# One weight block in four unsplit at the head of the channel mixers, and the norm's bias added later

## The chip, the cores and the metric

The kernel runs on one core of a Trainium2 chip, in one launch. The metric is the device time of the launch in microseconds, the median of the runs shown. TensorE multiplies matrices, DVE (VectorE) and POOL (GpSimd) work elementwise, ACT (ScalarE) applies functions, scales and biases, and SP issues the DMAs. Each engine works through its own queue in order.

## The reference

Two decoder layers over 256 tokens of width 2048, all in float32. Every sub-layer ends in `x = LayerNorm(alpha * x + sublayer(x))`, `LayerNorm(x) = (x - mean) / sqrt(var + eps) * g + b`. What matters here is the border between a mixer and the channel mixer that follows it:

```
x = layer_norm(ALPHA * x + mixer(x), ln1_g, ln1_b)
gate, val = x @ w_gate, x @ w_val            # 2048 -> 5632 each
h = silu(causal_dwconv(gate, conv_w) + conv_b) * val
x = layer_norm(ALPHA * x + h @ w_down, ln2_g, ln2_b)
```

## The kernel before

**Layout.** Activations lie feature-major: 16 tiles of 128 features x 256 tokens. The residual is `xf[0..15]` in float32. Weights come from memory as one stream per phase, in 128x128 blocks in the order of use; a chunk is eight blocks (512 KB), loaded by one DMA on SP's queue into one of three buffers (tag `wr`, L251).

**Three passes.** A float32 product is made of three TensorE passes in the faster type float32r. Each operand is split exactly into two parts, w = hi + lo and x = xh + xl, and a block is `hi xh + lo xh + hi xl` (`mac`, L350 to L354). `Stream.take` splits half a chunk (four blocks, 512 columns) at a time: ACT copies it to `wh` (L261), DVE or POOL subtracts to get `wl` (L265). There are four buffers of each. A raw buffer is free again when both its halves are split.

**The end of a mixer.** `out_part(..., last=True)` adds the last rows of the output projection to the residual (L848), tile by tile, and for each tile `ln_tile` (L402) takes the square on ACT, the sum of x on POOL (`accE`, L415) and the sum of the squares on DVE (`accQ`, L416). `ln_sums` (L420) then sums over the partitions with one-column matmuls (`lnst`, L433), gets 1/std on DVE, and spreads mean and 1/std over the partitions (`lnb`).

**The lead.** So as not to wait for these sums, the first nine groups of the channel mixer (`LEADS = 9`: a group of four column blocks, gate and value, then eight of one; 192 weight blocks in each layer) multiply the input before its LayerNorm, scaled by g: `raw(i)` makes the split of g x (`rawh` on ACT, L531; on POOL g x again, L534, and `rawl`, L535), with g and b in two more columns, so these matmuls have 258 columns. `plain` (L547) turns each result into that of the normalised input, with two DVE operations and two of ACT. Meanwhile `apply(i)` (L475) normalises the 16 tiles for the groups behind the lead: POOL subtracts the mean (L469), DVE multiplies by g and 1/std (L470) and adds the bias into the residual (`shift`, L473), ACT makes `xh` (L480) and POOL `xl` (L481). Two of these stand in each of the later lead groups (`PACE`), ordered behind the weight splits issued before them.

**What sets the order.** The program is written in the order of the code, and a planner reorders the instructions of each engine before the launch by modelled times and priorities; `tc.high_priority` moves the sums and the residual forward. On the chip each engine then keeps that order. In the lead, one in four of the splits goes to POOL (`LWL = "vvvp"`), after the first group.

**Behind the lead** come 38 column groups of gate and value blocks on `xh`, `xl`, each with the convolution (L636 to L638), the gate (L639, L640) and a split of the hidden tile (L324, L325), and then the down projection (`psd`), which adds to the residual (L656).

Of the kernel before, what the change touches and what calls it, by code (L numbers as in the profile page):

```python
# [9 lines left out]
F32 = mybir.dt.float32  # L10
# [6 lines left out]
P = 128  # L17
# [12 lines left out]
# ------------------------------------------------------------------ weight streams  # L30
# Each phase reads its weights as one stream of 128x128 blocks in the order of use.
# [93 lines left out]
# ------------------------------------------------------------------ small parameters  # L125
# [43 lines left out]
# ------------------------------------------------------------------ constants of the shapes  # L169
# [59 lines left out]
# ------------------------------------------------------------------ the program  # L229
class Stream:  # L230
    """The weights of a phase, in blocks of 128x128 in the order of use, split exactly into two parts
    of 12 significant bits: w = hi + lo."""
# [7 lines left out]
    def take(self, w, kt, key, n=1):  # L240
# [13 lines left out]
        if r == 0:  # L254
            self.hi = k.wpool.tile([P, self.HALF * P], F32R, name=f"wh_{self.name}_{c}_{g}", tag="wh", bufs=k.NWS)
            self.lo = k.wpool.tile([P, self.HALF * P], F32R, name=f"wl_{self.name}_{c}_{g}", tag="wl", bufs=k.NWS)
        sub = k.SUB.get(self.name, self.HALF)
        if r % sub == 0:
            a = slice(r * P, (r + sub) * P)
# [11 lines left out]
class K:  # L271
# [7 lines left out]
    # ---- set-up  # L279
# [25 lines left out]
    def need(self, kt, ahead=1):  # L305
        """Emit what makes tiles up to kt of the phase's input, and a few beyond."""
        while self.make_x and KT - len(self.make_x) <= kt + ahead:
            self.make_x.pop(0)()
# [21 lines left out]
    def phase(self, ctx, name, **banks):  # L330
        """The PSUM banks of a phase, by use."""
# [17 lines left out]
    # ---- three passes of exactly split operands  # L349
    def mac(self, out, hi, lo, xh, xl, first, last):  # L350
        mm = self.nc.tensor.matmul
        mm(out, hi, xh, start=first, stop=False)  # L352
        mm(out, lo, xh, start=False, stop=False)  # L353
        mm(out, hi, xl, start=False, stop=last)  # L354
# [11 lines left out]
    # ---- s -> 1/sqrt(s)  # L366
# [6 lines left out]
    def rsqrt_half(self, pool, h, n, name, ch=0):  # L373
        """h = -s / 2 -> 1/sqrt(s)."""
# [12 lines left out]
    # ---- residual + LayerNorm, feature-major  # L387
    def ln_start(self, name):
# [3 lines left out]
        if name[0] == "m":  # L392
            raw = self.lnctx.enter_context(self.tc.tile_pool(name=f"raw_{name}", **right))
            self.raw = [raw.tile([P, KT, T + 2], F32R, name=f"raw{n}_{name}") for n in "hl"]
        self.lnsum = ExitStack()
# [6 lines left out]
    def ln_tile(self, name, i):  # L402
        """Sums of x and x^2 over the feature tiles but for the last few, which ln_finish adds."""
# [16 lines left out]
    def ln_sums(self, name):  # L420
        """-> the mean and 1 / std of each token, spread over the partitions; yields between the two steps."""
# [4 lines left out]
        # the means of x and x^2 over the features, for the two halves of the tokens  # L426
# [23 lines left out]
        with hp(self.HP):  # L450
            v.tensor_copy(mean, st[0])
            # var = max(E[x^2] - mean^2, 0) + eps
# [10 lines left out]
    def ln_finish(self, name, gname, bname, final=False):  # L463
# [11 lines left out]
        def apply(i):  # L475
            h, l = self.xh[i], self.xl[i]
            scaled(i, nc.gpsimd)
            if name[0] == "m":
                shift(i)
                nc.scalar.activation(h, self.xf[i], AF.Copy)  # L480
                nc.gpsimd.tensor_tensor(l, self.xf[i], h.bitcast(F32), ALU.subtract)  # L481
                return
            nc.scalar.activation(h, self.xf[i], AF.Identity, bias=self.p(bname, i))
            v.scalar_tensor_tensor(l, self.xf[i], self.p(bname, i), h.bitcast(F32), ALU.add, ALU.subtract)
            if i == KT - 1:
                self.lead_done()
# [36 lines left out]
        # The products that come first take g x, before its LayerNorm, with g and b in two more columns  # L523
        rh, rl = self.raw
        gb = self.p(gname, 0, 2 * KT).rearrange("p (a k) -> p k a", a=2)
        nc.scalar.activation(rh[:, :, T:], gb, AF.Copy)
        v.tensor_tensor(rl[:, :, T:], gb, rh[:, :, T:].bitcast(F32), ALU.subtract)

        def raw(i):
            h, l = rh[:, i, :T], rl[:, i, :T]  # L530
            nc.scalar.activation(h, self.xf[i], AF.Copy, scale=self.p(gname, i))  # L531
            if i % 4 in self.RAWP:
                t = self.lnp.tile([P, T], F32, name=f"lnr_{name}_{i}", tag="lnr", bufs=2)
                nc.gpsimd.tensor_scalar(t, self.xf[i], self.p(gname, i), 1.0, ALU.mult, ALU.mult)  # L534
                nc.gpsimd.tensor_tensor(l, t, h.bitcast(F32), ALU.subtract)  # L535
            else:
                v.scalar_tensor_tensor(l, self.xf[i], self.p(gname, i), h.bitcast(F32), ALU.mult, ALU.subtract)
# [9 lines left out]
        def plain(o, i):  # L547
            """From W (g x), W g and W b to W (g (x - mean) / std + b)."""
# [7 lines left out]

        def end():
            self.need(KT)

# [15 lines left out]
    RAWP = (0, 1, 2, 3)  # L575

    def lead(self, st, keys, outs):
        """Products of the input of the FFN; the first few are of the input before its LayerNorm, so that they
        do not wait for its sums."""
# [8 lines left out]
        for kt in range(KT):  # L588
# [10 lines left out]
            for (w, key), o in zip(keys, outs):  # L599
                hi, lo = st.take(w, kt, key)  # L600
                self.mac(o[:, :T + 2], hi, lo, self.raw[0][:, kt], self.raw[1][:, kt], kt == 0, kt == KT - 1)
# [6 lines left out]
    def lead_done(self):  # L608
        """The temporaries of lead may go."""
# [4 lines left out]
    # ---- ConvGLU channel mixer  # L614
    def ffn(self, l):
# [3 lines left out]
        with ExitStack() as ctx:  # L619
# [5 lines left out]
            for grp in ffn_groups(l):  # L625
                outs = [self.bank("mm", f"ps_{w}_{c}") for w, c in grp]
                ps.update(zip(grp, self.lead(st, grp, outs)))
                for (w, c) in grp:
# [11 lines left out]
                    v.tensor_tensor(m, s, u, ALU.mult)  # L640
                    if c == FT // 2:
# [18 lines left out]
    # ---- rotary tables for 64-wide heads, two heads to a tile  # L660
    def rope_tables(self, tile):
        """tile(name, dtype) gives the temporaries."""
# [1034 lines left out]
```

## Time and profile before

| | |
|---|---|
| median of 3 runs | 2561.82 us (2561.67 to 2564.18) |
| profiled execution, first to last instruction | span 2556.7 us |
| what lies around the span, by the median | 5.1 us |
| busy share of the span: PE, DVE, ACT, POOL | 96%, 68%, 52%, 21% |
| mean granted TensorE clock | 0.982 of full speed |
| lead of layer 0 | 531.92 to 627.28 us |
| lead of layer 1 | 1769.65 to 1862.16 us |

The page gives no other time of the profiled execution than its span. The busy shares are means over the whole span; the lead is under a tenth of it, and there the shares are others. A matmul's own length in the trace (0.28 us) holds its way through the array; matmuls overlap, and the pace is the distance from start to start.

### The profile page before, as it was taken

What the parts mean: (1) busy time and instruction counts of PE and PEld (TensorE: products, weight loads), DVE (VectorE), ACT (ScalarE), POOL (GpSimd) and SP (SyncE); (2) the same over time, 40 slices, a digit from 0 to 9 for tenths busy, and PEclk for the clock granted to TensorE, in tenths of its full rate; (3) what the DMA queues carried; (4) which work ended last, traced back from release to release, by engine and by line L of the source; (5) the groups of instructions that cost most, each with busy time, mean ns of one, the idle gap of its engine ahead of it and who ended that gap; (6) DMA issues with size and microseconds to landing.
All of it is one profiled execution on the core that took longest, in us unless ns stands there. A gap on an engine that the chain in (4) does not pass through costs nothing.

```text
span 2556.7 us, 52762 instructions
## 1 busy us (share of the span) xinstructions
PE 2447.7 (96%) x20612; PEld 2362.1 (92%) x20612; DVE 1737.3 (68%) x3579; ACT 1328.5 (52%) x2577; POOL 535.8 (21%) x656
## 2 busy tenths in 40 slices
PE   8999999888999999999979999998899999999997
PEld 7888888778999999999979888998899999999996
DVE  6777667769666666555578787758976666665555
ACT  6455454355555555544445454445555555554443
POOL 3333343275000000000044233237500000000001
PEclk9999999989999999999989999999999999999998
DMA  6332333334555555555534444544355555555553
GB/s 214 128 99 89 110 98 117 110 101 147 191 189 190 190 187 187 187 190 190 190 126 147 139 135 146 186 163 159 124 190 190 190 186 188 189 190 190 188 188 128
DMA packets 129417, 412.13 MB, mean 161 GB/s; under 512 B 25488, under 2 KB 30224, under 8 KB 129168
## 3 DMA queue, kind: packets, MB, share of 16 engines
q1 hardware_dynamic: 129168, 408.77, 48.9%
q8 instruction: 161, 2.64, 0.4%
q14 instruction: 88, 0.72, 0.1%
HBM read 405.04 MB, written 2.10 MB: 159 GB/s over the span
## 4 chain that ended last, share of the span: by engine, by line
PE 81%; DVE 11%; issue 2%; DMA 2%; ACT 2%; POOL 1%; SPq 1%; DVEq 0%; ACTq 0%; POOLq 0%
PE psd L353 6%; PE psd L352 6%; PE psd L354 6%; PE ps_l_ffn_w_val L353 6%; PE ps_l_ffn_w_val L354 6%; PE ps_l_ffn_w_val L352 6%; PE ps_l_ffn_w_gate L354 6%; PE ps_l_ffn_w_gate L352 6%; PE ps_l_ffn_w_gate L353 6%; PE pso L352 2%; PE pso L353 2%; PE pso L354 2%; DVE wl_m L265 1%; DVE xf L470 1%; DVE wl_f L265 1%
## 5 line engine op out<-in xcount | busy, mean ns | idle before, releaser
L265 DVE TENSOR_TENSOR wl_f<-wr_f,wh_f 128x512 fp32r<-128x512 f32 x1040 | 744.8, 717 | 523.7 <-ACT wh_f L261 523.1
L261 ACT ACTIVATE wh_f<-wr_f 128x512 fp32r<-128x512 f32 x1056 | 665.8, 632 | 639.0 <-PE psd L354 232.8
L261 ACT ACTIVATE wh_m<-wr_m 128x512 fp32r<-128x512 f32 x464 | 289.8, 629 | 251.4 <-PE pso L354 78.4
L353 PE MATMUL psd<-hh,wl_f 128*128 128x256 f32 x1408 | 393.0, 279 | 0.0
L352 PE MATMUL psd<-hh,wh_f 128*128 128x256 f32 x1408 | 392.8, 279 | 0.0
L354 PE MATMUL psd<-hl,wh_f 128*128 128x256 f32 x1408 | 392.8, 279 | 0.0
L352 PE MATMUL ps_l_ffn_w_gate<-xh,wh_f 128*128 128x256 f32 x1216 | 339.2, 279 | 0.0
L354 PE MATMUL ps_l_ffn_w_gate<-xl,wh_f 128*128 128x256 f32 x1216 | 339.2, 279 | 0.0
L353 PE MATMUL ps_l_ffn_w_val<-xh,wl_f 128*128 128x256 f32 x1216 | 339.2, 279 | 0.0
L354 PE MATMUL ps_l_ffn_w_val<-xl,wh_f 128*128 128x256 f32 x1216 | 339.2, 279 | 0.0
L353 PE MATMUL ps_l_ffn_w_gate<-xh,wl_f 128*128 128x256 f32 x1216 | 339.2, 279 | 0.0
L352 PE MATMUL ps_l_ffn_w_val<-xh,wh_f 128*128 128x256 f32 x1216 | 339.2, 279 | 0.0
L265 POOL TENSOR_TENSOR wl_m<-wr_m,wh_m 128x512 fp32r<-128x512 f32 x154 | 215.0, 1396 | 374.3 <-ACT wh_m L261 308.7
L265 DVE TENSOR_TENSOR wl_m<-wr_m,wh_m 128x512 fp32r<-128x512 f32 x310 | 222.2, 719 | 75.7 <-ACT wh_m L261 68.4
L353 PEld LDWEIGHTS psd<-hh,wl_f 128*128 128x128 f32 x1408 | 264.7, 188 | 0.0
L354 PEld LDWEIGHTS psd<-hl,wh_f 128*128 128x128 f32 x1408 | 264.7, 188 | 0.0
L352 PEld LDWEIGHTS psd<-hh,wh_f 128*128 128x128 f32 x1408 | 264.6, 188 | 0.0
L352 PEld LDWEIGHTS ps_l_ffn_w_val<-xh,wh_f 128*128 128x128 f32 x1216 | 228.6, 188 | 0.0
L353 PEld LDWEIGHTS ps_l_ffn_w_val<-xh,wl_f 128*128 128x128 f32 x1216 | 228.6, 188 | 0.0
L354 PEld LDWEIGHTS ps_l_ffn_w_val<-xl,wh_f 128*128 128x128 f32 x1216 | 228.6, 188 | 0.0
L353 PEld LDWEIGHTS ps_l_ffn_w_gate<-xh,wl_f 128*128 128x128 f32 x1216 | 228.6, 188 | 0.0
L352 PEld LDWEIGHTS ps_l_ffn_w_gate<-xh,wh_f 128*128 128x128 f32 x1216 | 228.6, 188 | 0.0
(637 smaller groups left out, 5578.4 us busy)
## 6 DMA issues: line engine op xcount, KB each, us to landing
wr_f<-w_f SPq DMA_DIRECT2D x526, 512.0 KB
wr_m<-w_m SPq DMA_DIRECT2D x230, 512.0 KB
xf<-x SPq DMA_DIRECT2D x7, 256.0 KB
rwl<-lora SPq DMA_DIRECT2D x8, 192.0 KB
rdt<-rdecay SPq DMA_DIRECT2D x4, 384.0 KB
y<-xf SPq DMA_DIRECT2D x5, 256.0 KB
wr_m<-w_m SPq DMA_DIRECT2D x4, 256.0 KB
wr_f<-w_f SPq DMA_DIRECT2D x4, 256.0 KB
```

The lines of the kernel that those rows point to most:

```text
L261: nc.scalar.activation(self.hi[:, a], raw, AF.Copy)
L265: i = eng.tensor_tensor(self.lo[:, a], raw, self.hi[:, a].bitcast(F32), ALU.subtract)
L352: mm(out, hi, xh, start=first, stop=False)
L353: mm(out, lo, xh, start=False, stop=False)
L354: mm(out, hi, xl, start=False, stop=last)
L470: v.scalar_tensor_tensor(self.xf[i], self.xf[i], self.p(gname, i), rb, ALU.mult, ALU.mult)
```

## The change

In the lead, every fourth block of a half chunk is not split. `take(..., whole=True)` returns the raw float32 block in the loaded chunk, and `mac` multiplies it in one matmul with float32 g x (`rawf`, a third tile of 16 x 258 columns). ACT and DVE or POOL split only the other three blocks, 384 columns.

`raw(i)` makes g x in float32 on ACT, then `rawh` from it on ACT, and POOL only subtracts. `apply(i)` has for both kinds of norm the same form: the bias goes into `xh` on ACT and into `xl` with one DVE operation, and no longer into the residual. The residual gets it from ACT in `late`, one tile for each column group from the 22nd on.

```
-    def take(self, w, kt, key, n=1):
+    def take(self, w, kt, key, n=1, whole=False):
...
+        if whole and r == self.HALF - 1:
+            return self.raw[:, (g * self.HALF + r) * P:(g * self.HALF + r + 1) * P], None
         sub = k.SUB.get(self.name, self.HALF)
         if r % sub == 0:
-            a = slice(r * P, (r + sub) * P)
+            a = slice(r * P, (r + sub - whole) * P)
...
-    def mac(self, out, hi, lo, xh, xl, first, last):
+    def mac(self, out, hi, lo, xh, xl, first, last, x=None):
         mm = self.nc.tensor.matmul
+        if lo is None:
+            mm(out, hi, x, start=first, stop=last)
+            return
...
+            self.rawf = raw.tile([P, KT, T + 2], F32, name=f"rawf_{name}")
...
         def apply(i):
             h, l = self.xh[i], self.xl[i]
             scaled(i, nc.gpsimd)
-            if name[0] == "m":
-                shift(i)
-                nc.scalar.activation(h, self.xf[i], AF.Copy)
-                nc.gpsimd.tensor_tensor(l, self.xf[i], h.bitcast(F32), ALU.subtract)
-                return
             nc.scalar.activation(h, self.xf[i], AF.Identity, bias=self.p(bname, i))
             v.scalar_tensor_tensor(l, self.xf[i], self.p(bname, i), h.bitcast(F32), ALU.add, ALU.subtract)
-            if i == KT - 1:
+            if name[0] == "f" and i == KT - 1:
                 self.lead_done()
...
+        nc.scalar.activation(rf[:, :, T:], gb, AF.Copy)
...
         def raw(i):
-            h, l = rh[:, i, :T], rl[:, i, :T]
-            nc.scalar.activation(h, self.xf[i], AF.Copy, scale=self.p(gname, i))
-            if i % 4 in self.RAWP:
-                t = self.lnp.tile([P, T], F32, name=f"lnr_{name}_{i}", tag="lnr", bufs=2)
-                nc.gpsimd.tensor_scalar(t, self.xf[i], self.p(gname, i), 1.0, ALU.mult, ALU.mult)
-                nc.gpsimd.tensor_tensor(l, t, h.bitcast(F32), ALU.subtract)
-            else:
-                v.scalar_tensor_tensor(l, self.xf[i], self.p(gname, i), h.bitcast(F32), ALU.mult, ALU.subtract)
+            f, h, l = rf[:, i, :T], rh[:, i, :T], rl[:, i, :T]
+            nc.scalar.activation(f, self.xf[i], AF.Copy, scale=self.p(gname, i))
+            nc.scalar.activation(h, f, AF.Copy)
+            nc.gpsimd.tensor_tensor(l, f, h.bitcast(F32), ALU.subtract)
...
+        def late(i):
+            nc.scalar.activation(self.xf[i], self.xf[i], AF.Identity, bias=self.p(bname, i))
+
         def end():
             self.need(KT)
+            self.late = [lambda i=i: late(i) for i in range(KT)]
...
-                hi, lo = st.take(w, kt, key)
-                self.mac(o[:, :T + 2], hi, lo, self.raw[0][:, kt], self.raw[1][:, kt], kt == 0, kt == KT - 1)
+                hi, lo = st.take(w, kt, key, whole=True)
+                self.mac(o[:, :T + 2], hi, lo, self.raw[0][:, kt], self.raw[1][:, kt], kt == 0, kt == KT - 1,
+                         self.rawf[:, kt])
...
+                    if c >= FT // 2 and self.late:
+                        self.late.pop(0)()
```

## Rows read from the trace of the kernel before

**Rows 1.** The page's first part: busy us, share of the span, instructions.

```profile
PE 2447.7 (96%) x20612; PEld 2362.1 (92%) x20612; DVE 1737.3 (68%) x3579; ACT 1328.5 (52%) x2577; POOL 535.8 (21%) x656
```

**Rows 2.** Stretches: length, busy us (instructions) by engine, clock, DMA share, GB/s.

```profile
565.00:625.00 60.00, 50.23 (x385) 47.01 (x384) 59.08 (x94) 35.90 (x85) 39.55 (x38) 1.00 0.40 132
1800.00:1860.00 60.00, 52.87 (x397) 49.79 (x395) 58.54 (x95) 35.84 (x85) 37.94 (x38) 0.97 0.42 137
531.00:560.00 29.00, 23.86 (x169) 23.25 (x170) 15.47 (x34) 9.96 (x20) 24.58 (x30) 0.88 0.40 128
...
640.00:660.00 20.00, 20.00 (x174) 20.00 (x173) 12.39 (x22) 11.23 (x20) 0.00 (x0) 1.00 0.61 205
```

**Rows 3.** Timeline of PE at the lead's begin and end: start, length.

```profile
531.92 0.28 PE L352 MATMUL ps_l_ffn_w_gate<-rawh_m,wh_f 128*128 128x258 f32 x1
...
532.28 0.28 PE L352 MATMUL ps_l_ffn_w_val<-rawh_m,wh_f 128*128 128x258 f32 x1
...
627.28 0.28 PE L352 MATMUL ps_l_ffn_w_gate<-xh,wh_f 128*128 128x256 f32 x1
```

**Rows 4.** Timeline of PE at the norm's sums, idle time before in brackets.

```profile
552.80 1.01 PE L433 MATMUL lnst_m<-cb,accE_m 128*128 128x1 f32 x4 [4.49 <-POOL accE_m L415]
...
556.23 0.56 PE L352 MATMUL ps_l_ffn_w_gate<-rawh_m,wh_f 128*128 128x258 f32 x1
...
1786.91 0.61 PE L433 MATMUL lnst_m<-cb,accE_m 128*128 128x1 f32 x4 [3.79 <-POOL accE_m L415]
```

**Rows 5.** A stretch of 3 us behind that wait, columns as above.

```profile
556.00:559.00 3.00, 3.00 (x15) 3.00 (x16) 1.57 (x8) 0.63 (x1) 0.00 (x0) 0.50 0.00 0
```

**Rows 6.** Timeline of PE: two float32 matmuls among split ones, layer 1.

```profile
1389.49 1.02 PE L1419 MATMUL gq<-KQ 128*128 128x256 f32 x4
...
1390.47 0.28 PE L352 MATMUL psz<-xh,wh_m 128*128 128x256 f32 x1
```

**Rows 7.** Weight loads of that line: ns min/median/max, first and last start.

```profile
L1419 PEld LDWEIGHTS gq<-KQ x16: 187/188/191, 1382.1 to 1523.4; 128*128 128x128 f32 x16
```

**Rows 8.** DVE by line, 565 to 625: busy us, mean ns, idle before.

```profile
L265 DVE TENSOR_TENSOR wl_f<-wr_f,wh_f 128x512 fp32r<-128x512 f32 x21 | 16.0, 771 | 0.0
L473 DVE TENSOR_SCALAR xf<-xf,pb 128x256 f32<-128x256 f32 x16 | 13.1, 821 | 0.0
L470 DVE SCALAR_TENSOR_TENSOR xf<-xf,pb,lnb_m 128x256 f32<-128x256 f32 x16 | 11.1, 696 | 0.8 <-ACT lnb_m L447 0.8
L637 DVE SCALAR_TENSOR_TENSOR fa<-lnp_m_l_ffn_w_gate,pb,fa 128x255 f32<-128x255 f32 x5 | 4.3, 861 | 0.0
...
L325 DVE TENSOR_TENSOR hl<-fm,hh 128x256 fp32r<-128x256 f32 x5 | 3.2, 633 | 0.0
```

**Rows 9.** DVE by line, 1800 to 1860.

```profile
L473 DVE TENSOR_SCALAR xf<-xf,pb 128x256 f32<-128x256 f32 x16 | 8.3, 520 | 0.1
```

**Rows 10.** POOL by line, 565 to 625.

```profile
L481 POOL TENSOR_TENSOR xl<-xf,xh 128x256 fp32r<-128x256 f32 x16 | 16.9, 1064 | 9.1 <-ACT xh L480 8.0 <-ACT lnuv_m_l_ffn_w_gate L551 1.1
```

**Rows 11.** Four lines: ns min/median/max, first and last start us.

```profile
L534 POOL TENSOR_SCALAR lnr_m<-xf,pb x16: 468/650/1432, 515.6 to 554.5; 128x256 f32<-128x256 f32 x16
...
L484 DVE SCALAR_TENSOR_TENSOR xl<-xf,pb,xh x16: 468/471/1509, 1314.9 to 1333.2; 128x256 fp32r<-128x256 f32 x16
...
L470 DVE SCALAR_TENSOR_TENSOR xf<-xf,pb,lnb_m x16: 471/476/1519, 565.4 to 621.3; 128x256 f32<-128x256 f32 x16
...
L265 DVE TENSOR_TENSOR wl_f<-wr_f,wh_f x21: 677/680/1216, 570.5 to 620.7; 128x512 fp32r<-128x512 f32 x21
```

**Rows 12.** Timeline of DVE: an undisturbed 256-column operation.

```profile
526.91 0.41 DVE L416 TENSOR_TENSOR accQ_m<-accQ_m,lnq_m 128x256 f32<-128x256 f32 x1
```

**Rows 13.** SP's issue of a weight load, and the stretch in which its data ends.

```profile
562.24 0.33 SPq L251 DMA_DIRECT2D wr_f<-w_f  x1
...
565.00:566.00 1.00, 1.00 (x10) 1.00 (x10) 0.62 (x2) 1.00 (x4) 0.13 (x1) 1.00 0.42 66
```

More of the change, by code (lines that the diff above doesn't have):

```diff
@@ L524, in ln_finish @@
         rh, rl = self.raw
+        rf = self.rawf
         gb = self.p(gname, 0, 2 * KT).rearrange("p (a k) -> p k a", a=2)
+        nc.scalar.activation(rf[:, :, T:], gb, AF.Copy)
         nc.scalar.activation(rh[:, :, T:], gb, AF.Copy)
@@ L574 @@
     FIND = (1, 2, 3, 4, 6, 8, 10, 12, 14, 15, 16)
-    RAWP = (0, 1, 2, 3)
     def lead(self, st, keys, outs):
```

## The prediction

> **What bounds the kernel now.** I read the totals first: TensorE is busy 96% of the span [rows 1]. That means that a microsecond is won only where TensorE stands still or runs slowly, and any extra TensorE work costs time everywhere else. So I next cut the span into stretches. In the body of a channel mixer, 20 us hold 174 matmuls and DVE works 12.4 of them: TensorE sets the pace, 0.115 us a matmul [rows 2]. The change touches another stretch, the first 192 weight blocks of each channel mixer (the lead, nine groups). It begins at 531.92 and ends at 627.28 in layer 0, 95.4 us [rows 3]. Its three matmuls of 258 columns a block need 0.36 us (531.92 to 532.28), so 192 blocks need 69 us. Some 26 us are lost, in two places.
>
> Place A is the LayerNorm's sums, at 531 to 565. POOL runs without a break there (24.6 of 29 us [rows 2], the rest is after its last sum). TensorE waits 4.49 us for the last sum of x (3.79 us in layer 1) [rows 4]; behind that wait its granted clock is 0.50, the 1.2 GHz level [rows 5], so the sixteen one-column matmuls take 3.4 us (552.80 to 556.23) and the blocks behind them run at half pace.
>
> Place B is the normalisation beside the other groups: 565 to 625 and, in layer 1, 1800 to 1860. DVE is busy 59.1 and 58.5 of 60 us, TensorE issues 385 and 397 matmuls where 500 would fit [rows 2]. Here DVE sets the end: every block needs its lo half from DVE's queue, in which the normalisation's work stands too.
>
> **The change part by part.** The terms are against the profiled execution: its span is 2556.7 us; the median of the runs, 2561.8, lies 5.1 us above the span, which I carry over unchanged.
>
> *TensorE.* Of 384 lead blocks 96 go unsplit. The matmul of two float32 operands is visible elsewhere: two of 256 columns are four instructions, and from their first to the second split matmul behind them are 0.98 us [rows 6]. Less one split matmul (0.12) that is 0.43 us each, 0.44 at 258 columns, against 0.36: +0.08 a block, +7.7 us over both layers where TensorE sets the pace. No further gap is seen at the switch. Both weight loads of such a pair take 188 ns, as any other [rows 7], and lie beside its matmuls. The Trainium skill, "TensorE: Matmul & The Clock Gate", section "Weight-path perf modes", says that the fast weight load is not used for FP32; its formula (128 columns at 1.2 GHz) gives an estimate of 107 ns for a load, and if those loads lay bare, 96 x 2 x 0.107 = 20.6 us would be added and the change would lose. The trace does not agree that they do: 0.98 us leaves them no room.
>
> *Splits on DVE and ACT.* They shrink from 512 to 384 columns. A 256-column subtraction takes 0.41 [rows 12], a 512-column one 0.68 [rows 11], so 384 take 0.55: -0.13 each at least, a quarter of the mean 0.771 (-0.19) at most. I take the first: 21 of them in B [rows 8], -2.8 us, 23 in layer 1, -3.1.
>
> *Normalisation.* The bias addition leaves DVE (16 x 0.821 = 13.1 us in layer 0, 16 x 0.520 = 8.3 in layer 1 [rows 8, 9]). In its place stands the three-operand subtraction that POOL did. The channel mixers' own LayerNorm has that form: median 471 ns, longest 1509 [rows 11]; the bounds are 16 x 0.471 = 7.5 and, at the mean of the scaling beside it [rows 8], 16 x 0.696 = 11.1. I take the middle, 9.3: -3.8 us in layer 0, +1.0 in layer 1.
>
> *POOL gets out of DVE's way.* POOL loses 16.9 us of xl subtractions [rows 10], of 39.6 busy in B. DVE's operations are long only at times: the scaling has a median of 476 ns, a mean of 696 and a longest of 1519 [rows 8, 11]. Time over the undisturbed length: 21 x 0.09 for splits, 16 x 0.22 for scalings, and 20 convolution and gating operations (861 the first, 633 the last group) over 0.47, 20 x 0.28; together 11 us. Bounds: all or none goes. I let it fall with POOL's busy time, 43%: -4.7 us a layer. The Trainium skill, "SBUF — State Buffer", section "SBUF: two separate sides", says why such a thing could be: DVE and GpSimd share one port pair as an exclusive lock, and a DVE operation with two SBUF inputs takes part in it against a GpSimd operation that reads SBUF. By that rule the new DVE subtraction is exposed as the old addition was, and could cost its upper bound; the 1509 ns in rows 11 agrees.
>
> *B together.* DVE: 59.1 - 2.8 - 3.8 - 4.7 = 47.8 us, and 58.5 - 3.1 + 1.0 - 4.7 = 51.7. TensorE for the same 128 and 132 blocks: three quarters at 0.36, one at 0.44, 48.6 and 50.2 us. The two are now equal, so what is late next is TensorE itself, and two in-order queues with equal work never overlap fully. I choose 10% over the larger: 53.5 and 56.9, a gain of 6.5 + 3.1 = 9.6 us. Ends: no such loss, 19.7; 20%, -0.3.
>
> *A.* POOL loses the scaling of each tile, 16 with a median of 0.65 us [rows 11], over 10 us of the chain that ends in the late sum. It can't all come off: the place of the sums in TensorE's order is planned from modelled times, which see POOL shorten as well, so the wait may only move forward. All of it is worth 4.5 + 1.7 (the sums at full clock) + 1.5 (blocks at half pace, half of the 3 us in rows 5) = 7.7 us in layer 0, 6.8 in layer 1; none is the other end. I take a third, 4.8, less 31 whole blocks x 0.08 = 2.5: -2.3 us net (-12 to +2.5).
>
> *Costed at nothing.* ACT gets 16 more copies a layer for the unscaled split (about 0.4 us each). They lie in 531 to 560, where ACT is busy 10 of 29 us [rows 2]; without that cover 16 x 0.4 = 6.5 us a layer. The 16 late bias additions on ACT stand one to a column group in the body, where ACT works 11.2 of 20 us [rows 2] and nothing reads the residual until the down projection; without cover 16 x 0.5 = 8 us. Nothing of layer 1's input waits for them. No DMA is moved.
>
> *A wait is added.* A raw chunk (three buffers) was free when its split was done; now also TensorE must have passed its eighth block. Behind that wait stand only later weight loads on SP's queue. Issue to landing: issued at 562.24, the transfer ends in 565 to 566 [rows 13], 3 us. Round trip: 3.0 + hi 0.6 + lo 0.6 + the chunk itself (6 x 0.36 + 2 x 0.44 = 3.0) = 7.3 us in the time of three chunks, 9.1. 1.8 us are spare; I cost it at nothing.
>
> Sum: -9.6 - 2.3 = -11.9; 2556.7 - 11.9 + 5.1 = 2549.9, so 2550 us.
>
> **The rivals.**
> *The sums' wait goes, and the queues overlap well.* For it: POOL's chain loses more than twice the wait. Against: the planned order. -19.7 - 12 = -31.7 us: 2530.
> *DVE's relief is eaten.* For it: DVE's long operations may come from the POOL work that stays (the mean subtractions and the split in four), and equal queues stall. B gives nothing (+0.3), A +2.5 to -2: 2561 to 2565, no change that can be told. Against: at least 2.8 and 3.1 us of splits are gone for certain.
> *Slower: the raw chunk is held too long.* Mechanism: the late load holds ACT's hi split, that holds DVE's in-order queue, and with it the normalisation. It decides once queueing on ACT and DVE passes the spare 1.8 us a round. In B, DVE has 94 instructions in 60 us, so a split stands behind several of 0.5 to 0.9; with 4 us of queueing each chunk takes (4 - 1.8)/3 = 0.73 us longer, over the 32 chunks of B +23 us. With the -11.9: +11, 2573. For it: prefetch sinks from four chunks ahead to two. Against: while DVE is the slow one, a chunk takes over 3.6 us (60 us for 16), so the round has more slack, not less.
>
> **How the numbers follow.** Chances: the forecast 0.48 (2540 to 2557), the better overlap 0.18, the eaten relief 0.18, the held chunk 0.16. Under 0.2%, 5 us, a measurement of this kernel can't tell a difference: faster is below 2556.7, slower above 2566.9. Faster: 0.46 + 0.18 + 0.06 = 0.70; no change: 0.02 + 0.10 + 0.03 = 0.15; slower: 0.02 + 0.13 = 0.15. The range runs from 2531 (most of the first rival's best) to 2566, and leaves out the held chunk and a little below, 0.2.
>
> **What would show it.** Right: the lead shorter than 95.4 us in both layers; DVE under 90% busy in B with more matmuls in it; whole blocks 0.43 to 0.45 us apart; the additions of the bias on ACT after the lead. Wrong: ACT waiting for weight loads in the lead and SP waiting for TensorE (held chunk); DVE still 98% busy at the old pace (eaten relief); a wait for the sums longer than 4.5 us, with more time at the 1.2 GHz level; any difference outside the mixers' ends and leads, which nothing here explains.

## The result, and the profile after

| | before | after |
|---|---|---|
| median of the runs | 2561.82 us, 2563.0 with the run beside after | 2534.89 us (2533.39 to 2542.54, 4 runs) |
| ratio | | 0.9895, 95% interval 0.9882 to 0.9908 |
| profiled execution, span | 2556.7 us | 2532.2 us (time 2534.57) |
| lead of layer 0: first group, the rest | 34.5, 60.9 us | 32.7, 51.6 us |
| lead of layer 1: first group, the rest | 33.0, 59.5 us | 27.7, 52.3 us |

The change saves 27 us, where 12 were forecast. The lead's lengths are starts on TensorE's timeline; its first group ends where the 65th of the 192 blocks begins. They add to 187.9 us before and 164.2 after: 23.7 of the 24.5 us between the two spans. What is left lies around the spans. Before's median lies 5.1 us above its profiled span, after's profiled time 2.4 above its own. In all later executions of before, for which time and span are known one by one, the time is 1.7 to 2.9 us above the span. So the 5.1 is not what lies around a span: the profiled execution of before was some 2 to 3 us shorter than its median.

In some executions, of several kernels, TensorE issues some 1% fewer matmuls through a whole channel-mixer body (851 instead of 860 in 100 us at clock 1.00, shown at the end; called a slow body below), some 6 to 8 us a layer, so the experiments are read from their leads' lengths first and from medians second.

The page's first part (busy us, share of the span, instructions) answers to [rows 1]:

```profile
PE 2445.3 (97%) x20516; PEld 2357.9 (93%) x20516; DVE 1713.9 (68%) x3579; ACT 1338.7 (53%) x2643; POOL 483.5 (19%) x592
```

Stretches of after (length; busy us and instructions of PE, PEld, DVE, ACT, POOL; clock, DMA share, GB/s): the rest of the lead in both layers, and the 5 us with the clock at its lowest in layer 0 and their counterpart in layer 1. They answer to [rows 2, 5].

```profile
562.03:613.59 51.56, 49.89 (x355) 46.56 (x353) 48.09 (x95) 39.98 (x100) 21.92 (x22) 1.00 0.49 164
1784.82:1837.11 52.29, 50.22 (x354) 46.36 (x353) 46.74 (x95) 39.90 (x101) 22.51 (x22) 1.00 0.47 161
545.00:550.00 5.00, 5.00 (x24) 5.00 (x25) 2.68 (x15) 0.52 (x1) 0.19 (x1) 0.50 0.18 70
1770.00:1775.00 5.00, 5.00 (x40) 4.83 (x39) 2.32 (x5) 1.27 (x3) 1.11 (x2) 1.00 0.61 200
```

In layer 0 TensorE is now busy 49.9 of 51.6 us beside groups 2 to 9, against 50.2 of 60 before, and POOL 21.9 us instead of 39.6. The timeline of PE at the lead's begin and end and at the sums, answering to [rows 3, 4]:

```profile
529.34 0.36 PE L358 MATMUL ps_l_ffn_w_gate<-rawh_m,wh_f 128*128 128x258 f32 x1
...
542.87 0.61 PE L440 MATMUL lnst_m<-cb,accE_m 128*128 128x1 f32 x4 [2.47 <-POOL accE_m L422]
...
613.59 0.47 PE L358 MATMUL ps_l_ffn_w_gate<-xh,wh_f 128*128 128x256 f32 x1
...
1757.15 0.28 PE L358 MATMUL ps_l_ffn_w_gate<-rawh_m,wh_f 128*128 128x258 f32 x1
...
1764.81 0.61 PE L440 MATMUL lnst_m<-cb,accE_m 128*128 128x1 f32 x4 [0.54 <-POOL accE_m L422]
...
1837.11 0.47 PE L358 MATMUL ps_l_ffn_w_gate<-xh,wh_f 128*128 128x256 f32 x1
```

The sums stand 13.5 and 7.7 us behind the lead's begin (20.9 and 17.3 before), and still the waits shrank from 4.49 and 3.79 us to 2.47 and 0.54. In layer 0 the clock falls to 0.50 behind the wait as before. In layer 1 it stays at 1.00, where before it stood at 0.50 over this stretch:

```profile
1788.00:1794.50 6.50, 6.50 (x31) 6.50 (x32) 3.28 (x16) 0.92 (x2) 1.24 (x3) 0.50 0.02 4
```

Half of those 6.5 us and 3.3 us less of waiting, less what the unsplit blocks add, are about the 5.3 us that the first group gained there.

An unsplit block among split ones, on PE's timeline:

```profile
600.95 0.28 PE L360 MATMUL ps_l_ffn_w_val<-rawl_m,wh_f 128*128 128x258 f32 x1
601.07 0.60 PE L356 MATMUL ps_l_ffn_w_val<-rawf_m,wr_f 128*128 128x258 f32 x2
601.31 0.47 PE L358 MATMUL ps_l_ffn_w_gate<-rawh_m,wh_f 128*128 128x258 f32 x1
601.62 0.28 PE L359 MATMUL ps_l_ffn_w_gate<-rawh_m,wl_f 128*128 128x258 f32 x1
```

From 601.07 to the second split matmul behind it are 0.55 us; less one split matmul (0.12) that is 0.43, as forecast from [rows 6]. Its two weight loads have a median of 189 to 192 ns, close to the 188 in [rows 7].

DVE by line in layer 0, 562.03 to 613.59 (busy us, mean ns, idle before), answering to [rows 8]:

```profile
L268 DVE TENSOR_TENSOR wl_f<-wr_f,wh_f 128x384 fp32r<-128x384 f32 (+1 forms) x24 | 17.3, 738 | 2.7 <-ACT wh_f L264 2.7
L477 DVE SCALAR_TENSOR_TENSOR xf<-xf,pb,lnb_m 128x256 f32<-128x256 f32 x14 | 8.5, 609 | 0.0
L486 DVE SCALAR_TENSOR_TENSOR xl<-xf,pb,xh 128x256 fp32r<-128x256 f32 x15 | 7.2, 482 | 0.2 <-ACT xh L485 0.2
...
L641 DVE SCALAR_TENSOR_TENSOR fa<-lnp_m_l_ffn_w_gate,pb,fa 128x255 f32<-128x255 f32 x5 | 3.1, 626 | 0.0
```

The new subtraction (L486) runs at 482 ns, near its shortest, where the old bias addition took 821. And in layer 1, the min/median/max of the same lines from 1785 to 1837, to set beside [rows 11]:

```profile
L268 DVE TENSOR_TENSOR wl_f<-wr_f,wh_f x23: 545/551/1093, 1788.0 to 1836.7; 128x384 fp32r<-128x384 f32 x22, 128x512 fp32r<-128x512 f32 x1
...
L477 DVE SCALAR_TENSOR_TENSOR xf<-xf,pb,lnb_m x14: 471/476/951, 1790.4 to 1831.3; 128x256 f32<-128x256 f32 x14
...
L486 DVE SCALAR_TENSOR_TENSOR xl<-xf,pb,xh x15: 472/476/958, 1785.4 to 1832.4; 128x256 fp32r<-128x256 f32 x15
```

### The profile page after: what moved, and what is told of

Same layout as the page of the kernel before. It is cut to its first block, busy times and chain, and to the rows that moved or that the text cites. A ratio compares the mean times of both kernels' runs of the same rounds, so it can differ in the third digit from the quotient of the medians.

```text
span 2532.2 us, 52523 instructions
## 1 busy us (share of the span) xinstructions
PE 2445.3 (97%) x20516; PEld 2357.9 (93%) x20516; DVE 1713.9 (68%) x3579; ACT 1338.7 (53%) x2643; POOL 483.5 (19%) x592
## 4 chain that ended last, share of the span: by engine, by line
PE 82%; DVE 9%; DMA 2%; ACT 2%; issue 2%; POOL 2%; SPq 1%; POOLq 0%; ACTq 0%; DVEq 0%
PE psd L358 6%; PE psd L359 6%; PE psd L360 6%; PE ps_l_ffn_w_val L359 6%; PE ps_l_ffn_w_val L360 6%; PE ps_l_ffn_w_gate L360 6%; PE ps_l_ffn_w_val L358 6%; PE ps_l_ffn_w_gate L359 6%; PE ps_l_ffn_w_gate L358 6%; PE pso L358 2%; PE pso L359 2%; PE pso L360 2%; DVE wl_m L268 2%; PE rbig L1147 1%; DVE wl_f L268 1%
## 5 line engine op out<-in xcount | busy, mean ns | idle before, releaser
L268 DVE TENSOR_TENSOR wl_f<-wr_f,wh_f 128x512 fp32r<-128x512 f32 (+1 forms) x1040 | 736.6, 710 | 530.3 <-ACT wh_f L264 530.2
L264 ACT ACTIVATE wh_f<-wr_f 128x512 fp32r<-128x512 f32 (+1 forms) x1056 | 652.9, 621 | 633.4 <-PE psd L360 233.5
L360 PEld LDWEIGHTS ps_l_ffn_w_gate<-xl,wh_f 128*128 128x128 f32 x1216 | 228.6, 188 | 0.0
```

What stands on the lines that cost most here:

```text
L264: nc.scalar.activation(self.hi[:, a], raw, AF.Copy)
L268: i = eng.tensor_tensor(self.lo[:, a], raw, self.hi[:, a].bitcast(F32), ALU.subtract)
```

## The experiments

Lead lengths in us from each profiled execution, first group / rest; medians with the ratio to the kernel before, run on the same chip (its medians there were 2561.77 for e1 to e4, 2562.51 for e5 to e8 and 2562.17 for e9 to e12).

| kernel | layer 0 | layer 1 | sum | median | ratio, 95% |
|---|---|---|---|---|---|
| e1: unsplit blocks, old normalisation | 32.7 / 58.5 | 26.9 / 56.7 | 174.8 | 2544.4 | 0.9934, 0.9919 to 0.9949 |
| e2: new normalisation alone | 34.8 / 54.8 | 34.2 / 54.8 | 178.6 | 2553.0 | 0.996, 0.9947 to 0.9973 |
| e3: g x on ACT alone | 33.3 / 59.1 | 32.0 / 59.1 | 183.5 | 2562.1 | 0.9993, 0.9981 to 1.0005 |
| e4: own load for unsplit blocks | 31.8 / 51.2 | 31.5 / 51.0 | 165.6 | 2535.5 | 0.9891, 0.9877 to 0.9906 |
| e5: 16 more POOL operations | 32.7 / 58.3 | 28.5 / 59.8 | 179.4 | 2547.9 | 0.994, 0.9926 to 0.9955 |
| e6: one more pass per unsplit block | 32.6 / 54.4 | 29.0 / 55.6 | 171.6 | 2546.0 | 0.9939, 0.9918 to 0.9959 |
| e7: two in four unsplit | 31.3 / 53.5 | 27.9 / 54.2 | 167.0 | 2547.9 | 0.9939, 0.9919 to 0.9959 |
| e8: a third of the splits on POOL | 31.1 / 53.6 | 31.7 / 53.3 | 169.7 | 2543.9 | 0.9923, 0.9902 to 0.9945 |
| e9: unsplit in the first group only | 31.1 / 55.5 | 27.0 / 55.2 | 168.7 | 2555.5 | 0.9971, 0.9958 to 0.9983 |
| e10: unsplit behind it only | 34.9 / 51.3 | 32.0 / 51.4 | 169.6 | 2542.0 | 0.9919, 0.9896 to 0.9942 |
| e11: the mean's subtraction on DVE | 31.1 / 50.9 | 27.0 / 49.7 | 158.7 | 2539.0 | 0.9897, 0.9876 to 0.9919 |
| e12: and all lead splits on DVE | 31.1 / 48.5 | 26.9 / 48.3 | 154.8 | 2531.1 | 0.9878, 0.986 to 0.9896 |

A part of the first groups' differences is the clock alone. In layer 0 it stands at 0.50 for 6.8 us in after, e1, e4, e5 and e10 and for 3.4 us in e3, e6 to e9, e11 and e12; after, e5, e8, e11 and e12 have the same matmuls in the first group, and it takes 32.7 us at 6.8 and 31.1 us at 3.4. So some 1.6 us of a lead's difference to that of after can come from this.

### The parts alone: e1, e2, e3

e1 is the kernel after with the old normalisation:

```
         def apply(i):
             scaled(i, nc.gpsimd)
+            if name[0] == "m":
+                shift(i)
+                nc.scalar.activation(h, self.xf[i], AF.Copy)
+                nc.gpsimd.tensor_tensor(l, self.xf[i], h.bitcast(F32), ALU.subtract)
+                return
...
-            self.late = [lambda i=i: late(i) for i in range(KT)]
+            self.late = []
```

> The unsplit block and the new g x on ACT, but the normalisation as before (bias added into the residual by DVE, xl subtracted on POOL, nothing late). Theory 1 (what the change won came from DVE and POOL getting out of each other's way in the normalisation; the smaller splits give only their own 3 us a layer, TensorE's extra passes take 2.5 back where it sets the pace): 2552 to 2558 us, 5 to 11 below before, DVE still over 95% busy in the later lead groups and its scalings still at a mean of 650 to 750 ns. Theory 2 (the unsplit block is what carries the change, since DVE has a quarter less splitting): 2540 to 2547.

e2 is the kernel before without the five lines from `if name[0] == "m"` to `return` and with the late bias additions; raw(i) and the splits are as before.

> The kernel before with only the normalisation changed: bias into xh on ACT and into xl on DVE, residual's bias late on ACT; all blocks split, g x as before. Theory 1: 2544 to 2550 us, 13 to 19 below before, DVE's scalings fall to a mean of 550 to 620 ns and the late groups of the lead from 61 to 54 us or less. Theory 2: 2555 to 2560. POOL's chain in front of the norm's sums stays as it was, so the wait for the sums stays at about 4 us a layer.

e3 is e1 with every block split:

```
-                hi, lo = st.take(w, kt, key, whole=True)
+                hi, lo = st.take(w, kt, key)
```

> The kernel before with only g x made on ACT (a float32 copy, then its hi part) and one POOL operation for a tile in place of two; all blocks split, normalisation as before. Theory 1 and theory 2 both put the first group and the lead's start here: 2555 to 2560 us, 3 to 8 below before, the wait for the sums shorter than 4.5 and 3.8 us. If the planner only moves the sums forward (as the prediction feared): 2561 to 2564, no change, with a wait as long as before.

e1 gave 2544.4, in theory 2's range; e2 2553.0, between the two. So neither part is the change: by the leads, e1 is worth 13.1 us and e2 9.3, together 22.4 of the 23.7. e3's time did not move, though its lead is 4.4 us shorter: its profiled execution has one of the slow bodies (from the end of the lead of layer 0 to the begin of that of layer 1 it takes 1150.6 us, before 1142.4). Whether that is so in its other runs is not shown. The theory that the moved bias carries the gain falls; so does its opposite.

### The held raw chunk: e4

```
+        if whole and r == 0:
+            q = g * self.HALF + self.HALF - 1
+            self.wq = k.wqpool.tile([P, P], F32, ..., tag="wq", bufs=8)
+            nc.sync.dma_start(self.wq, self.dram[c][:, q * P:q * P + P])
         if whole and r == self.HALF - 1:
-            return self.raw[:, (g * self.HALF + r) * P:(g * self.HALF + r + 1) * P], None
+            return self.wq, None
```

> The changed kernel, but each unsplit block comes once more by its own 64 KB load into a buffer of its own (eight of them), so TensorE no longer holds the raw chunk. If the held chunk costs nothing because the round trip has slack (as the prediction costed it): 2533 to 2537 us, same as the changed kernel within 0.1%. If it costs what ACT waits for loads in the lead of layer 0 (6.2 us in eight waits): 2523 to 2529. If the extra loads on SP's queue delay the others: above 2538.

2535.5 against 2534.9, in the first range; lead 165.6 against 164.2. TensorE's hold on the chunk costs nothing that can be seen.

### What POOL's work costs DVE: e5, e11, e12

e5 adds 16 POOL subtractions a layer whose results nothing reads:

```
+            if name[0] == "m":
+                junk = self.lnx.tile([P, T], F32, ..., tag="junk", bufs=1)
+                nc.gpsimd.tensor_tensor(junk, self.xf[i], h.bitcast(F32), ALU.subtract)
```

> The kernel after, with 16 more POOL subtractions of 256 columns a layer, in the normalisation beside groups 2 to 9 (about 1 us each, their results unused), so POOL has as much to do there as it had before. Theory 1 (POOL's work lengthens DVE's operations, so a good part of the gain was POOL falling away): before, some 11 us of lengthening stood beside 39.6 us of POOL; 16 us more would give DVE back 4 to 5 us a layer, on top of 46.9 us busy in the 50 us of layer 0: DVE passes TensorE's 48.6 and the time rises by 2 to 4 us a layer, 2539 to 2543. Theory 2 (what counted is that DVE and ACT have less to do): nothing waits for these subtractions and the time stays at 2533 to 2537, with DVE's mean durations unchanged.

e11 takes the mean's subtraction off POOL, and e12 the lead's splits too:

```
-            scaled(i, nc.gpsimd)
+            scaled(i, nc.gpsimd if name[0] == "f" else v)
...
-    LWL = "vvvp"
+    LWL = "v"
```

> The kernel after, with the subtraction of the mean in the mixers' normalisation on DVE instead of POOL: 14 POOL operations of 0.99 us leave groups 2 to 9 of layer 0 (13.6 us), and 14 operations of some 0.47 us are added to DVE (6.6 us). Theory 1 (POOL's work lengthens DVE's, by 8.3 us for 14.3 us of POOL in the run that added POOL subtractions, 0.58 us per us): DVE loses 7.9 us of lengthening and gains 6.6, its busy time stays near 46 us, the scalings' mean falls from 609 to about 500 ns, and the time stays at 2531 to 2537. Theory 2 (the added POOL subtractions cost time because the normalised tiles came late in POOL's queue, and DVE's lengthening is small): DVE has 6 us more to do, 53 us, passes TensorE's 48.6 and the time rises by 4 to 6 us a layer, 2543 to 2547.

> As the run with the mean's subtraction on DVE, and the lead's splits too are all on DVE, so POOL does nothing beside groups 2 to 9. Theory 1 (lengthening comes from POOL): every DVE operation there has its shortest length, the mean of a group equal to its median (scaling 0.47, 384-column split 0.55): 32 x 0.55 + 3 x 16 x 0.47 + some 13 us for the rest = 53 us of DVE against TensorE's 48.6; 3 to 5 us a layer longer than after, 2540 to 2545. Theory 2 (the lengthening has another source, such as DMA writes or ACT): the means stay at 0.58 to 0.74 us, DVE reaches 60 us, 2555 or more.

The rest of the lead in e5, layer 0 and 1, and in e12 (columns as above):

```profile
558.98:617.30 58.32, 51.99 (x355) 46.55 (x353) 55.25 (x94) 40.26 (x100) 36.24 (x37) 1.00 0.42 145
1788.63:1848.48 59.85, 52.37 (x355) 46.28 (x353) 55.12 (x95) 40.55 (x101) 34.88 (x37) 1.00 0.42 141
```

```profile
567.14:615.61 48.47, 48.47 (x355) 46.63 (x353) 46.71 (x117) 38.15 (x97) 0.00 (x0) 1.00 0.54 174
1790.30:1838.59 48.29, 48.29 (x355) 46.47 (x353) 47.23 (x118) 38.72 (x98) 0.00 (x0) 1.00 0.53 174
```

And the scalings of layer 0 (ns min/median/max) in e5 and in e12:

```profile
L477 DVE SCALAR_TENSOR_TENSOR xf<-xf,pb,lnb_m x14: 472/956/981, 563.9 to 610.8; 128x256 f32<-128x256 f32 x14
```

```profile
L477 DVE SCALAR_TENSOR_TENSOR xf<-xf,pb,lnb_m x15: 474/477/486, 566.7 to 610.8; 128x256 f32<-128x256 f32 x15
L268 DVE TENSOR_TENSOR wl_f<-wr_f,wh_f x32: 545/550/683, 569.3 to 615.3; 128x384 fp32r<-128x384 f32 x30, 128x512 fp32r<-128x512 f32 x2
```

In e5 14.3 us more of POOL in layer 0 and 12.4 in layer 1 give DVE 7.2 and 8.4 us more (48.1 to 55.2, 46.7 to 55.1), and the lead's rest goes from 51.6 and 52.3 to 58.3 and 59.8: over both layers 0.58 us of DVE for each us of POOL. It cost more than theory 1 expected. DVE is not all of it: the lo halves that TensorE waits for in e5 are for the most part those that POOL makes, which now stand behind more work in POOL's own queue. In layer 0 it waits 4.9 us for POOL's and 1.3 for DVE's, in after 1.0 and 0.6; the longest rows of e5 are:

```profile
PE ps_l_ffn_w_val L359 <- POOL wl_f L268: 2.9, 4, 0.9
PE ps_l_ffn_w_gate L359 <- POOL wl_f L268: 2.0, 3, 1.0
```

In e12 the other way round: DVE takes over 14 mean subtractions and 8 splits and is busy 46.7 and 47.2 us, about as long as in after (48.1 and 46.7). With POOL silent no scaling is longer than 486 ns, and TensorE has no idle time in the stretch. I had expected e12 to be slower than after, from 13 us for DVE's other operations. By their lengths they take 18.4 us; what the sum left out is that on DVE one operation starts before the last one's end, as on its timeline in e12 (start, length):

```profile
581.77 0.48 DVE L477 SCALAR_TENSOR_TENSOR xf<-xf,pb,lnb_m 128x256 f32<-128x256 f32 x1
582.16 0.55 DVE L268 TENSOR_TENSOR wl_f<-wr_f,wh_f 128x384 fp32r<-128x384 f32 x1
582.63 0.42 DVE L476 TENSOR_TENSOR xf<-xf,lnb_m 128x256 f32<-128x256 f32 x1
```

From start to start each takes some 0.08 us less than its length (0.39 for 0.48, 0.47 for 0.55), some 9 us over all its operations there. Counted so, the 22 operations that DVE took over are 14 x 0.33 + 8 x 0.47 = 8.4 us, and POOL's 21.9 and 22.5 us in after had lengthened DVE by 9.8 and 7.9: an estimate of 0.35 to 0.45 us for each us of POOL, against 0.50 to 0.68 from e5. About a half is as exact as these runs are.

e11's median, 2539.0, is above theory 1's range; its profiled execution has a slow body in layer 0, and its lead is 5.5 us shorter than that of after. e12 is the shortest lead of all, 9.4 us under after, 7.1 of them behind the first group; its median, 2531.1 (2524.6 to 2535.7), is below both theories' ranges, and against 2534.9 it is not told apart by the intervals above.

By the Trainium skill, "SBUF — State Buffer", section "SBUF: two separate sides", DVE with two SBUF inputs and a GpSimd operation that reads SBUF exclude each other: one holds the shared port pair for its whole instruction, and the other waits. The two durations of the scaling in e5, 0.47 or about 0.96 us, and their collapse to one without POOL agree. So do two lines of before, 565 to 625 (ns min/median/max): the operation with its second tensor in PSUM is never lengthened, the one behind it, with both in SBUF, is.

```profile
L552 DVE SCALAR_TENSOR_TENSOR lnp_m_l_ffn_w_gate<-lnb_m,lnuv_m_l_ffn_w_gate,ps_l_ffn_w_gate x6: 468/470/482, 567.5 to 624.5; 128x256 f32<-128x256 f32 x6
L553 DVE SCALAR_TENSOR_TENSOR lnp_m_l_ffn_w_gate<-lnp_m_l_ffn_w_gate,lnb_m x5: 413/414/948, 569.7 to 610.6; 128x256 f32<-128x256 f32 x5
```

Why the lengthening comes in steps of about 0.5 us is not shown.

### Does TensorE set the pace now: e6, e7, e8

e6 multiplies once more behind each unsplit block (the hi part of g x by itself), and so adds to the result what the reference does not have:

```
-            mm(out, hi, x, start=first, stop=last)
+            mm(out, hi, x, start=first, stop=False)
+            mm(out, xh[:, :P], xh, start=False, stop=last)
```

> The kernel after, with one more float32r matmul of 258 columns (and its weight load) behind each of the 192 unsplit blocks; it adds a product that the reference doesn't have, only to load TensorE. Each costs 0.12 us of TensorE. (The lead of both layers has 384 blocks, 96 of them unsplit, so 96 x 0.12 = 11.5 us.) Theory 1 (TensorE sets the pace of the whole lead now, DVE's queue has room): all of it shows, 2544 to 2548. Theory 2 (DVE's queue still sets the pace beside groups 2 to 9): only the first group's 32 passes show, with what TensorE has too little slack for, 2537 to 2541.

e7 leaves two blocks of a half chunk unsplit (`r >= self.HALF - 2`, splits of 256 columns):

> The kernel after, with two blocks in four unsplit. TensorE gets 96 more of the longer blocks over both layers, 96 x 0.08 = 7.7 us; DVE's splits shrink from 384 to 256 columns, 44 x 0.13 = 5.7 us less. Theory 1 (TensorE sets the pace now): 5 to 8 us longer than after, 2540 to 2543. Theory 2 (the splits on DVE still set it): 3 to 6 us shorter, 2529 to 2532.

e8 has `LWL = "vvp"`:

> The kernel after, with POOL taking one in three of the lead's splits behind the first group where it took one in four. About 3 splits a layer leave DVE (3 x 0.74 = 2.2 us) and 3 of 1.1 us are added to POOL, which has 22 of 50 us to do. Theory 1 (TensorE sets the pace now): no difference, 2533 to 2537. Theory 2 (DVE's queue still sets it): 1.5 to 2 us shorter a layer, 2530 to 2532.

The rest of the lead in e6:

```profile
563.90:618.35 54.45, 53.78 (x386) 50.90 (x385) 48.25 (x95) 39.79 (x98) 22.22 (x22) 1.00 0.47 155
1790.96:1846.52 55.56, 53.99 (x386) 50.96 (x385) 48.37 (x95) 39.66 (x98) 22.04 (x22) 1.00 0.46 152
```

It grew by 2.8 and 3.3 us of 32 x 0.12 = 3.8, with DVE's busy time near what it was: most of what was added to TensorE shows. The median, 2546.0, is in theory 1's range. Theory 1 holds for groups 2 to 9: TensorE sets the pace there now, and DVE has some room. e7's time tells little, since both its bodies are slow; its lead is 2.8 us longer than after, between the theories. Behind the first group it takes 1.9 us more in both layers, though DVE is busy 43.0 and 43.3 us instead of 48.1 and 46.7; TensorE got 32 x 0.08 = 2.6 there. That is theory 1 again.

e8 tests nothing of this. Two or three splits a layer left DVE, but it was busy longer, 49.1 and 49.3 us instead of 48.1 and 46.7: beside a POOL with more to do (23.7 and 25.0 us) what stayed on DVE was longer. The rest of the lead grew by 2.0 and 1.0 us. Its median, 2543.9, is above both ranges; in its layer 1 the clock fell behind a wait of 1.38 us for the sums, and the first group took 4.0 us more than in after.

### Where the unsplit block pays: e9, e10

`whole=first` in e9, `whole=not first` in e10, for `whole=True`.

> The kernel after, with unsplit blocks in the first group alone (32 of 96 are left, over both layers); groups 2 to 9 split all four blocks. Theory 1 (the unsplit block pays in both places: a shorter first group of layer 1, where the sums come earlier and the clock stays up, and smaller splits beside groups 2 to 9): the lead behind its first group goes back to the 55 us of the kernel with the moved bias alone (50.5 and 52.5 in the kernel after), 4.5 + 2.6 us, 2540 to 2543. Theory 2 (it pays in the first group only): 2533 to 2536. Theory 3 (behind the first group only): 2549 to 2553.

> The kernel after, with unsplit blocks in groups 2 to 9 alone (64 of 96). Theory 1 (both places): groups 2 to 9 keep 50 to 53 us; the first group of layer 1 goes back from 27.5 to 32 to 34 us, with a wait for the sum of x of 2 us or more and a stretch of clock 0.50 behind it; 2539 to 2543. Theory 2 (first group only): 2549 to 2553. Theory 3 (groups 2 to 9 only): 2533 to 2536.

e9's rest goes back to 55.5 and 55.2 (e2: 54.8 and 54.8), and its first group of layer 1 stays at 27.0; e10 keeps 51.3 and 51.4 and loses the first group, 34.9 and 32.0, and its median, 2542.0, is in theory 1's range. So it pays in both places, theory 1. In e10's layer 1 TensorE waits for the sums (its timeline) and the clock falls (5 us behind it, columns as above):

```profile
1769.28 1.01 PE L440 MATMUL lnst_m<-cb,accE_m 128*128 128x1 f32 x4 [2.31 <-POOL accE_m L422]
```

```profile
1770.00:1775.00 5.00, 5.00 (x24) 5.00 (x24) 1.63 (x10) 0.18 (x1) 1.04 (x2) 0.50 0.36 118
```

e9's median, 2555.5, fits none of the three. Both its bodies are slow in the profiled execution, some 13 us against after, and 2555.6 less 13 would be in theory 1's 2540 to 2543. None of its twelve runs was under 2545.5; that they all have slow bodies is not shown. I let the lead decide, not the time.

Over all runs the first group of layer 1 takes 26.9 to 29.0 us where the clock stays at 1.00 behind the sums (after, e1, e5, e6, e7, e9, e11, e12) and 31.5 to 34.2 where it falls there (before, e2, e3, e4, e8, e10). The length of the wait does not alone decide it: after 1.35 us the clock stayed (e5), after 1.38 us it fell (e4, e8).

## Why the prediction was wrong

The direction and the place (both leads) held; the size did not: -11.9 us forecast, -24.5 between the two spans. Two terms were mis-sized. B, forecast at -9.6, measured -16.5: the surcharge for two equal queues was too large, and in layer 1 DVE's contention with POOL fell by far more than the 4.7 us put down for it. A, forecast at -2.3, measured -8.5: more came off the wait for the sums than the third that was chosen. (Behind the last lead 0.6 us were lost.) Point by point:

**B, layer 0.** DVE's sum was right: 47.8 forecast, 48.1 measured. What failed is the step behind it, "two in-order queues with equal work never overlap fully. I choose 10% over the larger". Measured, 51.6 us over a TensorE floor of 48.6 is 6%; the gain was 9.3 us, not 6.5 (0.9 of the difference is that the rest of the lead was 60.9 us long before, not the 60 of the stretch compared). PE's waits in the kernel after, 563 to 613 (total us, times, longest), come to 1.6 us for lo halves; before they were 8.8, all on DVE:

```profile
PE ps_l_ffn_w_val L359 <- POOL wl_f L268: 1.0, 2, 0.7
PE ps_l_ffn_w_gate L359 <- DVE wl_f L268: 0.4, 1, 0.4
PE ps_l_ffn_w_val L359 <- DVE wl_f L268: 0.2, 1, 0.2
```

What came, 9.3 + 7.2 = 16.5 us for both layers, lies between the 9.6 chosen and my "no such loss" end, 19.7, nearer to the end. What the surcharge stood for can be taken away: with POOL silent (e12) the loss is nil. How much of it is DVE's lengthening and how much POOL's own late splits (1.0 of the 1.6 us) is not separated; e11, in which TensorE waits for none of POOL's splits, still takes 50.9 and 49.7 us.

**B, layer 1.** Here DVE's sum was wrong, 51.7 forecast, 46.7 measured. Contention was to fall by 4.7 us, 0.28 us for each us of POOL; e5 and e12 put it at about a half, and POOL lost 14 us (17 in layer 0). By the lengths of its operations, splits and `plain` included, it fell by some 8.5. The new subtraction was to cost 9.3 us, the middle between undisturbed and disturbed; 16 at the measured mean of 0.509 are 8.1. So TensorE became the larger queue, by a margin; 52.3 us are 8% above its 48.6, and the gain was 7.2, not 3.1. Up to 1.7 us of it are the clock, which before stood at 0.50 once more in this part of the lead, for 3.4 us (0.97 over the stretch in [rows 2]), and nowhere in this part of after:

```profile
1829.00:1832.00 3.00, 3.00 (x16) 3.00 (x16) 3.00 (x7) 1.86 (x5) 1.53 (x2) 0.50 0.78 212
```

I took the 0.28 from operations whose shortest length I knew, and left out the bias addition, which was lengthened most. The kernel before, layer 0, 565 to 625 (ns min/median/max):

```profile
L473 DVE TENSOR_SCALAR xf<-xf,pb x16: 342/825/1387, 566.2 to 623.7; 128x256 f32<-128x256 f32 x16
```

It took 13.1 us instead of 16 x 0.342 = 5.5, though it reads one tensor only. With these 7.6 us, lengthening before was 11 + 7.6 = 18.6 us beside 39.6 of POOL, 0.47 for one, close to the two experiments. The row was there to be read.

**A.** -2.3 net was forecast. The lead of layer 0 began 2.6 us earlier and its first group gained 1.8; the stretch between the leads lost 1.2 and the first group of layer 1 gained 5.3, -8.5 in all. I took a third of the full prize because the planner might only move the wait forward. It did move the sums forward, but the wait shrank too, and in layer 1 so far that the clock did not fall. e3 (POOL's scaling gone, all blocks split) still waits 3.33 and 2.30 us, e10 (unsplit behind the first group) 3.32 and 2.31; with unsplit blocks in the first group and the rest as in after it is 2.47 and 0.54 (after), 2.47 and none (e9). That the rest comes from the unsplit blocks is shown; by which step of the planned order, not. How much the first group of layer 1 gains is not sure either: of the kernels with unsplit blocks in it, e4, e5 and e8 wait 1.35 to 1.38 us there, and in e4 and e8 the clock falls, which makes the group some 4 us longer. The lead's begin in layer 0 varies between 526 and 536 us over all kernels, so the 2.6 us there may be nothing.

**Around the span.** The 5.1 us carried over are not what lies around a span; in the profiled execution of after it is 2.4 us. That is 2.7 us of the miss.

**At nothing.** The held chunk cost nothing (e4), right. The late bias additions cost nothing that the spans show, but not where I put them: the planner moved all 16 of a layer into the lead itself, where ACT had room (40.0 of 51.6 us busy in layer 0). ACT's line in after, 529 to 614:

```profile
L558 ACT ACTIVATE xf<-xf,pb x16: 492/497/510, 558.5 to 610.0; 128x256 f32<-128x256 f32 x16
```

**The rivals.** What happened is near the first one, "the sums' wait goes, and the queues overlap well", 2530 at a chance of 0.18. Its two halves came as 16.5 of 19.7 us and 8.5 of 12. The relief was not eaten and the chunk not held too long. Two small sums of the prediction are off (the 6.8 in A is 3.8 + 1.7 + 1.5 = 7.0, the round trip of 7.3 adds up to 7.2); nothing hangs on them. Of the signs named for being right, DVE under 90% busy came in layer 1 (89%) and not in layer 0 (93%), and the late bias additions came inside the lead.

**Unsplit blocks and splits.** +0.08 us of TensorE a block was right (0.43 to 0.44). The split of 384 columns has a shortest length of 0.545 us, as estimated (0.55).

## What to carry to other kernels

Before adding up an engine's queue, read min, median and mean of each of its operations: a mean far above the minimum beside a busy neighbour is contention, and it goes with the neighbour's work, all operations counted. An operation given to a slow engine to relieve another can lengthen the other by half of what it takes itself, so moving it back may cost nothing. Where the larger of two queues is clear, expect its length and some per cent more (here 6 and 8, and nothing with POOL silent), and test by adding work to one queue at a time, looking at what each queue's busy time then does.

## What the runs showed of the hardware

Two float32 operands in one matmul of 258 columns take 0.43 us of TensorE, against 0.36 for three passes of float32r, with no gap at the switch.

DVE's scaling of 256 columns takes 0.47 us, or about 0.95, or 1.52, and nearly nothing between (before, layer 0: eleven of 16 at 0.47 to 0.49, three at 0.95 or 0.96, two at 1.52), and at most 0.486 with POOL silent. A median alone says little of such a queue. Operations in a row start some 0.08 us before the one ahead ends, so lengths added up are more than DVE's busy time.

Unexpected was the slow body. From 800 to 900 us in after, and in the bodies of both layers in e9 (columns as above):

```profile
800.00:900.00 100.00, 100.00 (x860) 100.00 (x859) 63.16 (x108) 55.49 (x98) 0.00 (x0) 1.00 0.57 187
```

```profile
800.00:900.00 100.00, 100.00 (x851) 100.00 (x850) 62.68 (x107) 55.44 (x98) 0.00 (x0) 1.00 0.59 189
1950.00:2050.00 100.00, 100.00 (x852) 100.00 (x851) 62.41 (x106) 54.76 (x98) 0.00 (x0) 1.00 0.58 186
```

TensorE waits for nothing, the granted clock is 1.00, and a matmul comes every 0.1175 us instead of 0.1163. Of the 28 bodies of the 14 profiled executions six are so (e3 and e11 layer 0, e7 and e9 both). No run here shows what decides it; it stays open.
